# Convolution taps, one product and three groups of TensorE work placed elsewhere in a two-layer mixer

## The chip, the cores and the metric

The kernel runs on one core of one Trainium2 chip. The metric is device time in microseconds (us), as the median of three runs. The engines are TensorE (PE in the profile, with PEld for its weight loads), VectorE (DVE), ScalarE (ACT), GpSimd (POOL) and SyncE (SP), which only issues DMAs here. Each engine works through its own instructions in the order in which the program gives them.

## What is computed

256 tokens of width 1024 go through two layers of a first block and one layer of a second. A layer of the first block is, cut to what matters here:

```
x = x + 0.5 * swiglu(rms_norm(x))                    # feed-forward, width 2816
proj = rms_norm(x) @ w_in
y_rwkv = rwkv7(token_shift(proj[:, :1280]))           # 6 heads of 64: a recurrence over tokens
y_attn = dilated_attention(q, k, v)                   # 6 heads, blocks of 128 keys
y_conv = conv(u)                                      # 256 channels
x = x + concat(y_rwkv, y_attn, y_conv) @ w_out
x = x + 0.5 * swiglu(rms_norm(x))

conv:  z = u[:, :256] * sigmoid(u[:, 256:])
       z = depthwise convolution of z, 31 taps, + bias      # causal, over tokens
       z = (z - mean(z)) * rsqrt(var(z) + 1e-5) * ln_w + ln_b
       y = silu(z)

rwkv7: state = state * w + (state @ -kk) x (kk * a) + v x k ;  y = state @ r     # for each token
       then a norm over each head, a bonus term, a gate
```

All of it is float32. The second block (attention, a short convolution, pooling, feed-forward) is not touched.

## The kernel before

A float32 product runs on TensorE as three passes: each weight piece of 128 x 1024 is loaded by SyncE (`raw`), copied by ScalarE into `hi` (L287), and VectorE makes `lo = raw - hi` (L288). A product is then `hi*xh + lo*xh + hi*xl`. There are three `raw` buffers and six each of `hi` and `lo`, so a piece's `hi` can only be written once TensorE has done with the piece six before it.

Inside a layer's mixer (`mixers`, L793) the token recurrence is turned into products over two chunks of 128 tokens. For each chunk and head a triangular system has to be solved. It is done in 16 x 16 blocks first (`substitute`, L1001): 15 steps of three small VectorE instructions each, a shuffle (L1004), a product (L1005) and a sum (L1007), each needing the one before. The result `X16` goes through ScalarE into `X32` (L1070, L1071) and through VectorE's transpose into `Y32` (L1072), and TensorE then joins the blocks into 32 x 32, 64 x 64 and 128 x 128 systems (`XM`, `A16`, `A32`, `A64`, `Yf`). In front of the substitution stand the products `Bt` and AR (L975 to L977) and their scores (L990), which make the system's matrix `XM`.

TensorE's gaps between these dependent pieces are filled with matmuls of the large projections. Each projection is a generator in the list `jobs`; `run(n)` (L810) advances it by n steps, of three matmuls each (`mm` in the profile). While the mixer is emitted, TensorE's matmuls are pinned to the order of the code (`pinned`, `tc.keep_in_program_order`). The order on VectorE, ScalarE, GpSimd and SyncE is not pinned: a scheduler chooses it by its own estimate of when operands are ready.

Names that the change touches, with their lines before:

- `taps(j)` (L865): for each of the two halves of the convolution's channels, 30 VectorE instructions (L869) that add one tap each to `ca[j]`, each needing the one before, with a ScalarE instruction at each end (L867, L870). The code calls it late (L1260), but its input `z` is ready early, so the scheduler spreads the taps over VectorE.
- `km` (L1075), a product of 128 x 768 on VectorE, and `Kt` (L1076), which is made of it.
- `turned(...)` (L1111): three transposes on TensorE of the values `vT`, copied by ScalarE to `Vt`. `vT` is written by VectorE at L841. `rv_of(0)` (L1163) multiplies `ka[0]` by `Vt`.
- `AR[:, :, :, 1]` (L1198), the receptance part; the scores `kr[0]` (L1230) need it.
- the convolution's tail: the channel sum `cs` (L1261), `csq` (L1268), `token_rsqrt` of it (L1285, with its power on GpSimd), `spread` over the tokens (L1293), and the tanh gate that gives `mix[6]` and `mix[7]`. The fourth output projection step group, `ojob(3)`, is the first that reads `mix[6]`.
- in the feed-forward (`Grouped.go`, L556): the hidden values of one column group are turned by TensorE (`turning`, L571) between the steps of the next group.

Of the kernel before, what the change touches and what calls it, by code (L numbers as in the profile page):

```python
# [14 lines left out]
OP = mybir.AluOpType  # L15

T, DM, ND = 256, 1024, 8
# [168 lines left out]
def tile_model(ctx, tc, A, at, out):  # L186
# [113 lines left out]
    def both(calls):  # L300

        for i, c in enumerate(calls):
            m = pe.matmul(*c[:3], start=c[3], stop=c[3] if len(c) < 5 else c[4], skip_group_check=True)
            if i or pinned[0]:
                tc.keep_in_program_order(m)

    def turn(ps, src):

        placed(pe.transpose(ps, src, ident))  # L309
# [200 lines left out]
    class Grouped:  # L510
# [45 lines left out]
        def go(self, finish, nxt, aside=None):  # L556
# [45 lines left out]
            for g, (c0, m) in enumerate(GROUPS):  # L602
                if g:

                    b, hs = self.space(m), []
                    t = turning(h, 512, hs)
                    for i, _ in enumerate(self.cols(b, m)):
                        if (i if m == 512 else i - 2) >= 0:
                            next(t, None)
                    for _ in t:  # L610
                        pass
                    s = silu(b, m)
                    if g == 2 and aside:
                        aside()
                    if m == 512:
                        downs(hs, g == 1)
# [176 lines left out]
    def mixers(me, finish, nxt):  # L793
        l, lpk, hl = me.l, me.lpk, me.nrm.hl

        def lpar(name, i=0, n=1, p0=0, p1=128):
            o, w = at[1][name]
            return lpk[p0:p1, o + i:o + i + n]
# [66 lines left out]
        def taps(j):  # L865
            ca[j] = tmp.tile([128, T], F32, name="ca", bufs=2)
            act.activation(ca[j], z[:, j, 30:], AF.Identity, scale=lpar("taps", j * TAPS + 30))  # L867
            for k in range(30):
                dve.scalar_tensor_tensor(ca[j], z[:, j, k:k + T], lpar("taps", j * TAPS + k), ca[j], op0=OP.mult, op1=OP.add)  # L869
            act.activation(ca[j], ca[j], AF.Identity, scale=0.5, bias=lpar("conv_dw_b", j))  # L870
# [115 lines left out]

        run(16)
        XM = [n6(t3("XM")) for c in range(2)]
# [9 lines left out]
        dve.tensor_scalar(N16, N32[:, :, 0:16], m0, None, op0=OP.mult)  # L998
        dve.scalar_tensor_tensor(N16, N32[:, :, 16:32], m1, N16, op0=OP.mult, op1=OP.add)

# [70 lines left out]
        act.activation(X32[:, :, 16:32], X16, AF.Copy, scale=m1)  # L1071
        dve.transpose(Y32, X32)  # L1072
        run(4)
        qk_spread(k_, 1.0, rbk)
        dve.tensor_tensor(km_[:, :768], km_[:, :768], kT_[:, :768], op=OP.mult)  # L1075
        dve.tensor_tensor(c4(Kt_), c4(km_), Ei[:, :, :, 1:129], op=OP.mult)  # L1076
# [61 lines left out]
        run(8)  # L1138
        turned(lambda f: vT[:, f, 0:128], Vt[:, 0])
        mix[3] = at_[0].out(vtok)  # L1140
# [11 lines left out]
        run(8)  # L1152
        turned(lambda f: vT[:, f, 128:256], Vt[:, 1])

# [8 lines left out]
        def rv_of(c):  # L1163
            b = bank("at")
            both([(b[:, hc], ka[c][:, h], Vt[:, c, hc], h == 0) for h, f, p, hc in heads])
            act.activation(Rv[c], b[:, :384], AF.Copy)

        rv_of(0)
        run(8)
        at_[1].turns()  # L1170
# [94 lines left out]
        for j in range(2):  # L1265
            dve.scalar_tensor_tensor(ca[j], cs[:, :T], -1.0 / 256, ca[j], op0=OP.mult, op1=OP.add)
            csq.append(t1("csq"))
            act.activation(csq[j], ca[j], AF.Square)  # L1268
        run(4)

        yc_ = u3("yc"); yc = v3(yc_)
# [8 lines left out]
        run(4)  # L1280
        b2 = bank("at")
        for j in range(2):
            for c in range(2):
                mm(b2[:, c:c + 1], csq[j][:, c * 128:c * 128 + 128], ones[:, 0:1], j == 0 and c == 0, j == 1)
        rc = token_rsqrt(b2[:, :2], 2, 1.0 / 256, 1e-5, "nc")  # L1285
        run(2)
        b = bank("at")
        head_sums(b, [ysq[:, f] for f in range(3)])
        rb_ = t3("rby"); rb = rb_[:, :768].rearrange("p (c n) -> p c n", c=2)
        head_rsqrt(b, 6, 1.0 / 64, 64e-5, rb, "nr")  # L1290
        run(2)
        rs = bank("at")[:, :T]
        spread(rs, rc)  # L1293
        for j in range(2):
# [5 lines left out]
            dve.scalar_tensor_tensor(yb, th, 1.0, yb, op0=OP.add, op1=OP.mult)  # L1300
            mix[6 + j] = split(yb, 0.5)

        Dc_ = u3("Dc"); Dc = v3(Dc_)
# [10 lines left out]
        dve.tensor_tensor(yc_[:, :768], yc_[:, :768], gw_[:, :768], op=OP.mult)  # L1314
        run(6)
        for f, ps in enumerate(spread3(rb)):
# [256 lines left out]
```

## Time and profile before

| what | value |
|---|---|
| device time, median of 3 runs | 1443.67 us (1442.15 to 1444.58) |
| the profiled execution's own time | 1440.27 us |
| its span, first to last instruction | 1438.5 us |
| mean granted TensorE clock | 0.971 |
| TensorE busy | 1373.0 us, 95% |
| VectorE busy | 887.7 us, 62% |
| ScalarE busy | 773.5 us, 54% |
| GpSimd busy | 59.7 us, 4% |

The shares are averages over stages. TensorE's idle time and its lowered clock stand almost wholly in two places, around 200 to 390 us and 760 to 940 us: the mixers of the two layers. The times of the two mixers agree within 0.1 us wait for wait, so the rows further down are of the first; the second layer's stand 556 us later. "Granted clock" is the share of full speed that the throttle allows: 1.00 is 2.4 GHz and 0.50 is 1.2 GHz. In a timeline the first column is the start, the second the duration, and the bracket at the end gives the idle time of that engine before the instruction and what ended it.

### The profile page before, as it was taken

How to read it: one execution, taken by the hardware profiler on the slowest of the kernel's cores; microseconds unless marked ns; L12 is line 12 of the kernel's file. 1: busy time of each engine (PE TensorE's matmuls, PEld its weight loads, DVE VectorE, ACT ScalarE, POOL GpSimd, SP SyncE). 2: the span in 40 equal slices, each digit the busy share in tenths (PEclk: the TensorE clock that was granted, in tenths of full speed). 3: DMA queues.
4: the chain of work that ended last, by engine and by line, in shares of the span. 5: the costliest groups of instructions: out<-in, count | busy, mean ns of one | idle time of the engine just before them, and what ended most of it. 6: DMA issues, size and time to landing. Idle time of an engine off the chain costs nothing. (4 is left out here: it accounts for less than half of the span.)

```text
span 1438.5 us, 24789 instructions
## 1 busy us (share of the span) xinstructions
PE 1373.0 (95%) x10034; PEld 1252.5 (87%) x10034; DVE 887.7 (62%) x1450; ACT 773.5 (54%) x1251; POOL 59.7 (4%) x72
## 2 busy tenths in 40 slices
PE   9999999689999999999999869999999999899997
PEld 7888999588888889888898859888889988899997
DVE  6555477865754656545566885664545556777765
ACT  5544455464643545444446545554444487766664
POOL 1000012000100000000002200110000000000000
PEclk9999999789999999999999969999999999999998
DMA  7756563321565764665663522266665534566551
GB/s 238 228 185 183 182 201 111 106 82 52 161 191 176 231 195 152 214 182 186 190 194 115 152 72 64 98 204 182 188 183 183 177 121 149 158 178 176 176 176 44
DMA packets 68658, 231.41 MB, mean 161 GB/s; under 512 B 7704, under 2 KB 12480, under 8 KB 68544
## 3 DMA queue, kind: packets, MB, share of 16 engines
q1 hardware_dynamic: 68544, 229.83, 52.0%
q8 instruction: 78, 1.28, 0.4%
q14 instruction: 36, 0.29, 0.1%
HBM read 227.69 MB, written 2.11 MB: 160 GB/s over the span
## 5 line engine op out<-in xcount | busy, mean ns | idle before, releaser
L288 DVE TENSOR_TENSOR lo<-raw,hi 128x1024 fp32r<-128x1024 f32 (+1 forms) x388 | 473.9, 1223 | 370.7 <-ACT hi L287 369.6
L287 ACT ACTIVATE hi<-raw 128x1024 fp32r<-128x1024 f32 (+1 forms) x388 | 407.7, 1054 | 450.5 <-PE at L298 204.4
L298 PE MATMUL mm<-hl,hi 128*128 128x256 f32 x880 | 248.9, 283 | 1.7 <-DVE hl L665 1.2
L298 PE MATMUL mm<-hh,lo 128*128 128x256 f32 x880 | 247.2, 281 | 0.0
L298 PE MATMUL mm<-hh,hi 128*128 128x256 f32 x880 | 247.1, 282 | 0.0
L298 PE MATMUL at<-hi,xh 128*128 128x512 f32 (+1 forms) x768 | 231.2, 382 | 0.1
L298 PE MATMUL at<-lo,xh 128*128 128x512 f32 (+1 forms) x768 | 224.0, 373 | 0.2
L298 PE MATMUL at<-hi,xl 128*128 128x512 f32 (+1 forms) x768 | 223.9, 373 | 0.0
L298 PEld LDWEIGHTS mm<-hl,hi 128*128 128x128 f32 x880 | 166.0, 189 | 5.5 <-DVE hl L665 4.7
L298 PEld LDWEIGHTS mm<-hh,hi 128*128 128x128 f32 x880 | 166.0, 189 | 1.6 <-issue 0.4
L298 PEld LDWEIGHTS mm<-hh,lo 128*128 128x128 f32 x880 | 166.2, 189 | 0.0
L298 PEld LDWEIGHTS at<-lo,xh 128*128 128x128 f32 x768 | 139.7, 188 | 27.4 <-DVE lo L398 1.3
L298 PEld LDWEIGHTS at<-hi,xl 128*128 128x128 f32 x768 | 140.0, 188 | 26.0
L298 PE MATMUL mm<-xh,hi 128*128 128x256 f32 x512 | 154.2, 301 | 2.5 <-ACT xh L481 2.5
L298 PEld LDWEIGHTS at<-hi,xh 128*128 128x128 f32 x768 | 132.8, 189 | 18.6 <-ACT hi L397 0.9
L298 PE MATMUL mm<-xl,hi 128*128 128x256 f32 x512 | 148.2, 289 | 0.5 <-DVE xl L482 0.5
L298 PE MATMUL mm<-xh,lo 128*128 128x256 f32 x512 | 147.9, 289 | 0.0
L298 PE MATMUL at<-xh,hi 128*128 128x256 f32 x432 | 123.1, 286 | 1.5 <-ACT xh L1521 1.5
L298 PE MATMUL at<-xl,hi 128*128 128x256 f32 x432 | 123.0, 286 | 0.6 <-DVE xl L425 0.6
L298 PE MATMUL at<-xh,lo 128*128 128x256 f32 x432 | 122.3, 284 | 0.0
L298 PEld LDWEIGHTS mm<-xh,hi 128*128 128x128 f32 x512 | 101.3, 198 | 7.4 <-ACT xh L481 3.3
L298 PEld LDWEIGHTS mm<-xl,hi 128*128 128x128 f32 x512 | 101.2, 198 | 2.1 <-DVE xl L482 0.9
(310 smaller groups left out, 1788.7 us busy)
## 6 DMA issues: line engine op xcount, KB each, us to landing
raw<-ffn SPq DMA_DIRECT2D x326, 512.0 KB, 3.6
raw<-win SPq DMA_DIRECT2D x60, 512.0 KB, 3.8
raw<-wout SPq DMA_DIRECT2D x24, 512.0 KB, 3.6
raw<-win SPq DMA_DIRECT2D x8, 384.0 KB, 3.1
raw<-ffn SPq DMA_DIRECT2D x8, 256.0 KB, 4.8
bias<-dbias SPq DMA_DIRECT2D x12, 128.0 KB, 2.2
lpk<-pack SPq DMA_DIRECT2D x2, 625.0 KB, 4.9
rows<-ebd SPq DMA_DIRECT2D x16, 64.0 KB, 2.8
```

The costliest lines, as they stand in the source:

```text
L287: act.activation(hi[:, :n], raw[:, :n], AF.Copy)
L288: dve.tensor_sub(lo[:, :n], raw[:, :n], hi[:, :n].bitcast(F32))
L298: placed(pe.matmul(out, lhsT, rhs, start=start, stop=stop, skip_group_check=True))
```

## The change

Five edits:

1. In the feed-forward, the transposes of the hidden values start two steps later in column group 1 and one step later in group 5.
2. The scores that make `XM` come after 18 steps of the projections instead of 16; the two steps come out of those that follow.
3. `behind(i, first)` gives the scheduler an order without a semaphore: the first tap of each half behind the transpose `Y32`, and the `km` product behind `N16`, the last preparation of the substitution.
4. The two `turned` calls of the values move one `run(8)` on, and `rv_of(0)` with its `run(8)` moves behind the second.
5. The sums of the convolution's squares and their factor move ahead of the head means of the recurrence; the head factor `rby` moves behind the convolution's gate, and two `run(2)` become part of a `run(9)`.

```diff
@@ -304,6 +304,11 @@
             if i or pinned[0]:
                 tc.keep_in_program_order(m)
 
+    def behind(i, first):
+
+        tc.add_manual_dep(i.ins, first.ins.name, mybir.DependencyInfo(mybir.DependencyClass.NoSync, mybir.DependencyReason.DATA),
+                          reason="behind")
+
     def turn(ps, src):
 
         placed(pe.transpose(ps, src, ident))
@@ -605,7 +610,7 @@
                     b, hs = self.space(m), []
                     t = turning(h, 512, hs)
                     for i, _ in enumerate(self.cols(b, m)):
-                        if (i if m == 512 else i - 2) >= 0:
+                        if i >= {1: 2, 5: 3}.get(g, 0):
                             next(t, None)
                     for _ in t:
                         pass
@@ -866,7 +871,9 @@
             ca[j] = tmp.tile([128, T], F32, name="ca", bufs=2)
             act.activation(ca[j], z[:, j, 30:], AF.Identity, scale=lpar("taps", j * TAPS + 30))
             for k in range(30):
-                dve.scalar_tensor_tensor(ca[j], z[:, j, k:k + T], lpar("taps", j * TAPS + k), ca[j], op0=OP.mult, op1=OP.add)
+                t = dve.scalar_tensor_tensor(ca[j], z[:, j, k:k + T], lpar("taps", j * TAPS + k), ca[j], op0=OP.mult, op1=OP.add)
+                if k == 0:
+                    behind(t, y32)
             act.activation(ca[j], ca[j], AF.Identity, scale=0.5, bias=lpar("conv_dw_b", j))
 
         def vjob():
@@ -984,7 +991,7 @@
             for hh in range(2):
                 dve.tensor_tensor(dst[:, hh::2], b[hh], smask[:, mk, None, :].to_broadcast([128, 3, 128]), op=OP.mult)
 
-        run(16)
+        run(18)
         XM = [n6(t3("XM")) for c in range(2)]
         for c in range(2):
             scores(c, Bt, 0, 0, XM[c])
@@ -996,7 +1003,7 @@
                 dve.transpose(N32[q, c * 6:c * 6 + 6], XM[c][q, :, q])
         N16 = i16("N16")
         dve.tensor_scalar(N16, N32[:, :, 0:16], m0, None, op0=OP.mult)
-        dve.scalar_tensor_tensor(N16, N32[:, :, 16:32], m1, N16, op0=OP.mult, op1=OP.add)
+        n16 = dve.scalar_tensor_tensor(N16, N32[:, :, 16:32], m1, N16, op0=OP.mult, op1=OP.add)
 
         def substitute():
             for s in range(15):
@@ -1069,10 +1076,10 @@
         X32, Y32 = half("X32", 12), half("Y32", 12)
         act.activation(X32[:, :, 0:16], X16, AF.Copy, scale=m0)
         act.activation(X32[:, :, 16:32], X16, AF.Copy, scale=m1)
-        dve.transpose(Y32, X32)
+        y32 = dve.transpose(Y32, X32)
         run(4)
         qk_spread(k_, 1.0, rbk)
-        dve.tensor_tensor(km_[:, :768], km_[:, :768], kT_[:, :768], op=OP.mult)
+        behind(dve.tensor_tensor(km_[:, :768], km_[:, :768], kT_[:, :768], op=OP.mult), n16)
         dve.tensor_tensor(c4(Kt_), c4(km_), Ei[:, :, :, 1:129], op=OP.mult)
         run(2)
         dbias = lambda h: A["dbias"][:, h * T:h * T + T]
@@ -1136,7 +1143,6 @@
             for q in qs:
                 act.activation(Yf[c][q, :, q], Y32[q, c * 6:c * 6 + 6], AF.Copy)
         run(8)
-        turned(lambda f: vT[:, f, 0:128], Vt[:, 0])
         mix[3] = at_[0].out(vtok)
         att_scores(1)
 
@@ -1150,7 +1156,7 @@
             act.activation(Yf[c][0:32, :, 32:64], b[0:32, c * 6:c * 6 + 6], AF.Copy)
             act.activation(Yf[c][64:96, :, 96:128], b[64:96, c * 6:c * 6 + 6], AF.Copy)
         run(8)
-        turned(lambda f: vT[:, f, 128:256], Vt[:, 1])
+        turned(lambda f: vT[:, f, 0:128], Vt[:, 0])
 
         for c in range(2):
             b = bank("at")[:, :384].rearrange("p (n j) -> p n j", n=6)
@@ -1165,8 +1171,9 @@
             both([(b[:, hc], ka[c][:, h], Vt[:, c, hc], h == 0) for h, f, p, hc in heads])
             act.activation(Rv[c], b[:, :384], AF.Copy)
 
+        run(8)
+        turned(lambda f: vT[:, f, 128:256], Vt[:, 1])
         rv_of(0)
-        run(8)
         at_[1].turns()
         for c in range(2):
             b = bank("at")[:, :384].rearrange("p (n j) -> p n j", n=6)
@@ -1267,6 +1274,11 @@
             csq.append(t1("csq"))
             act.activation(csq[j], ca[j], AF.Square)
         run(4)
+        b2 = bank("at")
+        for j in range(2):
+            for c in range(2):
+                mm(b2[:, c:c + 1], csq[j][:, c * 128:c * 128 + 128], ones[:, 0:1], j == 0 and c == 0, j == 1)
+        rc = token_rsqrt(b2[:, :2], 2, 1.0 / 256, 1e-5, "nc")
 
         yc_ = u3("yc"); yc = v3(yc_)
         ysq_ = t3("ysq"); ysq = v3(ysq_)
@@ -1278,17 +1290,6 @@
             dve.scalar_tensor_tensor(yc[:, f], ps[f], -1.0 / 64, yT[:, f], op0=OP.mult, op1=OP.add)
             act.activation(ysq[:, f], yc[:, f], AF.Square)
         run(4)
-        b2 = bank("at")
-        for j in range(2):
-            for c in range(2):
-                mm(b2[:, c:c + 1], csq[j][:, c * 128:c * 128 + 128], ones[:, 0:1], j == 0 and c == 0, j == 1)
-        rc = token_rsqrt(b2[:, :2], 2, 1.0 / 256, 1e-5, "nc")
-        run(2)
-        b = bank("at")
-        head_sums(b, [ysq[:, f] for f in range(3)])
-        rb_ = t3("rby"); rb = rb_[:, :768].rearrange("p (c n) -> p c n", c=2)
-        head_rsqrt(b, 6, 1.0 / 64, 64e-5, rb, "nr")
-        run(2)
         rs = bank("at")[:, :T]
         spread(rs, rc)
         for j in range(2):
@@ -1299,6 +1300,10 @@
             act.activation(th, yb, AF.Tanh, scale=0.5)
             dve.scalar_tensor_tensor(yb, th, 1.0, yb, op0=OP.add, op1=OP.mult)
             mix[6 + j] = split(yb, 0.5)
+        b = bank("at")
+        head_sums(b, [ysq[:, f] for f in range(3)])
+        rb_ = t3("rby"); rb = rb_[:, :768].rearrange("p (c n) -> p c n", c=2)
+        head_rsqrt(b, 6, 1.0 / 64, 64e-5, rb, "nr")
 
         Dc_ = u3("Dc"); Dc = v3(Dc_)
         gw_ = u3("gw"); gw = v3(gw_)
@@ -1312,7 +1317,7 @@
             dve.scalar_tensor_tensor(Dc[:, f], Dc[:, f], lpar("rwkv_ln_b", f), b[:, T:2 * T], op0=OP.add, op1=OP.mult)
             act.activation(gw[:, f], b[:, T:2 * T], AF.Identity, scale=lpar("rwkv_ln_w", f))
         dve.tensor_tensor(yc_[:, :768], yc_[:, :768], gw_[:, :768], op=OP.mult)
-        run(6)
+        run(9)
         for f, ps in enumerate(spread3(rb)):
             dve.tensor_tensor(yc[:, f], ps, yc[:, f], op=OP.mult)
             dve.tensor_tensor(yc[:, f], yc[:, f], Dc[:, f], op=OP.add)
```

Edit 3 shows on VectorE. At the end of the substitution (`X` is `X16`, `tb` its scratch, `ca` the taps), before:

```order
L1004 STREAM_SHUFFLE tb<-X_2103 128x12x14
L869 SCALAR_TENSOR_TENSOR ca<-z,lpk,ca 128x256
L1005 TENSOR_TENSOR tb<-tb,N_2365 128x12x14
L869 SCALAR_TENSOR_TENSOR ca<-z,lpk,ca 128x256
L1007 TENSOR_TENSOR X_2103<-X_2103,tb 128x12x14
L869 SCALAR_TENSOR_TENSOR ca<-z,lpk,ca 128x256
L1004 STREAM_SHUFFLE tb<-X_2103 128x12x15
L869 SCALAR_TENSOR_TENSOR ca<-z,lpk,ca 128x256
L1005 TENSOR_TENSOR tb<-tb,N_2365 128x12x15
L869 SCALAR_TENSOR_TENSOR ca<-z,lpk,ca 128x256
L1007 TENSOR_TENSOR X_2103<-X_2103,tb 128x12x15
L869 SCALAR_TENSOR_TENSOR ca<-z,lpk,ca 128x256 x3
```

and now, where line numbers are 7 higher for the substitution and 5 higher for the taps:

```order
L1011 STREAM_SHUFFLE tb<-X_2103 128x12x13
L288 TENSOR_TENSOR lo<-raw,hi 128x1024
L1012 TENSOR_TENSOR tb<-tb,N_2377 128x12x13
L288 TENSOR_TENSOR lo<-raw,hi 128x1024
L1014 TENSOR_TENSOR X_2103<-X_2103,tb 128x12x13
L1011 STREAM_SHUFFLE tb<-X_2103 128x12x14
L1012 TENSOR_TENSOR tb<-tb,N_2377 128x12x14
L1014 TENSOR_TENSOR X_2103<-X_2103,tb 128x12x14
L1011 STREAM_SHUFFLE tb<-X_2103 128x12x15
L1012 TENSOR_TENSOR tb<-tb,N_2377 128x12x15
L1014 TENSOR_TENSOR X_2103<-X_2103,tb 128x12x15
L1079 STREAM_TRANSPOSE Y_2670<-X_2669 128x384
```

The taps between the small instructions are gone; the first seven of them stand behind the transpose. Two weight splits (`lo`) stand between the small instructions instead, as others did before.

Further on VectorE, ahead of AR's second half (`r` is the receptance, `raws` its projection as it leaves PSUM), before:

```order
L836 TENSOR_TENSOR raws<-mm,R 128x2x256
L288 TENSOR_TENSOR lo<-raw,hi 128x1024
L841 SCALAR_TENSOR_TENSOR r<-raws,omu,m_3243 128x256
L841 SCALAR_TENSOR_TENSOR r<-raws,omu,m_3246 128x256
L836 TENSOR_TENSOR raws<-mm,R 128x256
L288 TENSOR_TENSOR lo<-raw,hi 128x1024
L841 SCALAR_TENSOR_TENSOR r<-raws,omu,m_3330 128x256
L479 TENSOR_TENSOR xl<-at,xh 128x256
L1198 TENSOR_TENSOR AR<-r,E 128x6x128
```

and now:

```order
L874 SCALAR_TENSOR_TENSOR ca<-z,lpk,ca 128x256 x2
L841 TENSOR_TENSOR raws<-mm,R 128x2x256
L874 SCALAR_TENSOR_TENSOR ca<-z,lpk,ca 128x256
L288 TENSOR_TENSOR lo<-raw,hi 128x1024
L846 SCALAR_TENSOR_TENSOR r<-raws,omu,m_3230 128x256
L846 SCALAR_TENSOR_TENSOR r<-raws,omu,m_3233 128x256
L874 SCALAR_TENSOR_TENSOR ca<-z,lpk,ca 128x256 x12
L841 TENSOR_TENSOR raws<-mm,R 128x256
L874 SCALAR_TENSOR_TENSOR ca<-z,lpk,ca 128x256 x2
L846 SCALAR_TENSOR_TENSOR r<-raws,omu,m_3330 128x256
L484 TENSOR_TENSOR xl<-at,xh 128x256
L1205 TENSOR_TENSOR AR<-r,E 128x6x128
```

Of the 60 taps of a layer, 15 stand in this piece now and none before.

Edit 4 shows on TensorE. Behind the last step of the projection of the values (`pk` with `v` is the transpose), before:

```order
L298 MATMUL mm<-xh,hi 128x256
L298 MATMUL mm<-xl,hi 128x256
L298 MATMUL mm<-xh,lo 128x256
L309 MATMUL at<-pk,v 128x128 x3
L303 MATMUL at<-PT,va 64x256 x2
L303 MATMUL at<-PT,va 64x128 x2
L303 MATMUL at<-ka,q 128x128 x2
L303 MATMUL at<-ka,q 128x256 x2
```

and now, at the same place:

```order
L298 MATMUL mm<-xh,hi 128x256
L298 MATMUL mm<-xl,hi 128x256
L298 MATMUL mm<-xh,lo 128x256
L303 MATMUL at<-PT,va 64x256 x2
L303 MATMUL at<-PT,va 64x128 x2
L303 MATMUL at<-ka,q 128x128 x2
L303 MATMUL at<-ka,q 128x256 x2
```

with the first transposes eight steps later, in front of the 64 x 64 systems:

```order
L298 MATMUL mm<-xl,hi 128x256
L298 MATMUL mm<-xh,lo 128x256
L314 MATMUL at<-pk,v 128x128 x3
L298 MATMUL at<-XA,XM 64x64 x12
L303 MATMUL at<-AR,Kt 128x128 x6
```

The attention output (`PT,va`) and the next scores (`ka,q`) follow the projection directly; the first transposes come behind the 32 x 32 systems and 24 more matmuls of a projection.

## Rows read from the trace of the kernel before

**Rows 1.** The page, part 1: busy us, share, instructions.

```profile
PE 1373.0 (95%) x10034; PEld 1252.5 (87%) x10034; DVE 887.7 (62%) x1450; ACT 773.5 (54%) x1251; POOL 59.7 (4%) x72
```

**Rows 2.** Waits of TensorE, whole span: line, what it waited for, us, times, longest.

```profile
PE at L298 <- ACT X L1070: 28.1, 2, 14.0
PE at L309 <- DVE v L841: 8.4, 2, 4.2
PE at L303 <- DVE Bt L976: 4.3, 2, 2.2
...
PE at L309 <- DVE sg L568: 2.3, 2, 1.6
```

**Rows 3.** Timeline of TensorE, 225 to 296 us: start, us, what, [idle before, releaser].

```profile
234.26 2.78 PE L303 MATMUL at<-AR,Bt 64*128 64x128 f32 x24 [2.16 <-DVE Bt L976]
...
280.21 1.48 PE L298 MATMUL at<-X,XM 32*32 32x16 f32 x96 [14.03 <-ACT X L1070]
```

**Rows 4.** Windows, TensorE alone: stretch, us, PE busy (instructions), granted clock, DMA.

```profile
230.02:231.82 1.80, 1.80 (x17) 1.00 0.00 0
...
234.30:237.90 3.60, 3.60 (x28) 0.53 0.28 56
...
280.20:285.50 5.30, 5.29 (x115) 0.50 0.04 8
...
300.50:309.60 9.10, 9.05 (x108) 0.50 0.40 143
...
353.80:360.50 6.70, 5.28 (x19) 0.75 0.07 11
```

**Rows 5.** Timeline of ScalarE, 225 to 330 us.

```profile
262.44 2.00 ACT L287 ACTIVATE hi<-raw 128x1024 fp32r<-128x1024 f32 x2
...
279.70 0.45 ACT L1070 ACTIVATE X<-X,pk 128x192 f32<-128x192 f32 x1 [12.72 <-DVE X L1007]
```

**Rows 6.** Groups of VectorE, 243.2 to 279.7 us: instructions, busy, mean ns, idle before.

```profile
L869 DVE SCALAR_TENSOR_TENSOR ca<-z,lpk,ca 128x256 f32<-128x256 f32 x30 | 14.2, 474 | 0.0
L288 DVE TENSOR_TENSOR lo<-raw,hi 128x1024 fp32r<-128x1024 f32 (+1 forms) x9 | 10.2, 1130 | 4.1 <-ACT hi L287 4.1
L1004 DVE STREAM_SHUFFLE tb<-X 128x12 f32<-128x12 f32 (+14 forms) x15 | 4.2, 277 | 0.0
...
L1007 DVE TENSOR_TENSOR X<-X,tb 128x12 f32<-128x12 f32 (+14 forms) x15 | 3.8, 250 | 0.0
```

**Rows 7.** Timeline of VectorE, 236 to 290 us.

```profile
243.28 0.21 DVE L1004 STREAM_SHUFFLE tb<-X 128x12 f32<-128x12 f32 x1
...
271.18 0.28 DVE L1005 TENSOR_TENSOR tb<-tb,N 128x132 f32<-128x132 f32 x1
271.38 0.47 DVE L869 SCALAR_TENSOR_TENSOR ca<-z,lpk,ca 128x256 f32<-128x256 f32 x1
271.78 0.28 DVE L1007 TENSOR_TENSOR X<-X,tb 128x132 f32<-128x132 f32 x1
...
281.27 2.40 DVE L869 SCALAR_TENSOR_TENSOR ca<-z,lpk,ca 128x256 f32<-128x256 f32 x5
```

**Rows 8.** Timeline of VectorE, 212 to 237 us.

```profile
228.24 0.96 DVE L1075 TENSOR_TENSOR km<-km,k 128x768 f32<-128x768 f32 x1 [2.13 <-ACT km L960]
```

**Rows 9.** Timeline of TensorE, 296 to 372 us.

```profile
300.55 0.48 PE L309 MATMUL at<-pk,v 128*128 128x128 f32 x1 [4.18 <-DVE v L841]
...
329.15 0.94 PE L303 MATMUL at<-AR,Kt 64*128 64x128 f32 x12
...
359.96 0.38 PE L298 MATMUL mm<-xh,hi 128*128 128x256 f32 x1 [1.27 <-ACT xh L481]
```

**Rows 10.** Windows, all engines: PE, PEld, DVE, ACT, POOL busy, clock, DMA.

```profile
279.70:300.50 20.80, 16.16 (x334) 14.74 (x334) 18.87 (x46) 14.65 (x36) 0.11 (x1) 0.83 0.15 43
300.50:327.90 27.40, 27.31 (x288) 24.10 (x289) 13.03 (x32) 15.63 (x38) 0.58 (x5) 0.83 0.26 86
327.90:346.40 18.50, 18.50 (x202) 16.35 (x202) 11.08 (x30) 8.49 (x23) 0.00 (x0) 1.00 0.24 72
```

## The prediction, made before the changed kernel was run

> **What bounds the kernel now.** I read the page's first part first. TensorE is busy 95% of the span and every other engine at most 62% [rows 1], so time is lost only where TensorE waits or runs slowly. The list of TensorE's waits comes next: the largest are two waits each (one a layer) of 14.0 us for `X32`, 4.2 us for `v` and 2.2 us for `Bt`, with a small one for the feed-forward's `sg` [rows 2]. TensorE's timeline puts them at their places [rows 3, 9]. The windows show what follows each: right behind the wait the granted clock is about 0.5, the lower of the two levels, for 3.6, 5.3 and 9.1 us [rows 4]. So a wait costs itself and part of the slow stretch behind it. Last I ask who is late: `X32` follows ScalarE's wait for VectorE's `X16` [rows 5], and VectorE from the first shuffle at 243.28 (the second instruction of the substitution's stretch, [rows 7]) to 279.7, where ScalarE takes `X16` over [rows 5], has no idle time but 4.1 us for `hi` [rows 6]. The stretch holds 45 small instructions (15 each of 4.2, 3.8 and, as long as the sums, 3.8 us of products, 11.8), 30 taps (14.2 us) and other work.
>
> The sums below are for one layer, made against the profiled execution (1440.27 us) and doubled; the median of the runs, 1443.67, lies 3.4 above it, and the saving is taken off that.
>
> **Bt and its scores (edits 2 and 3).** The `km` product stands in VectorE's queue ahead of `Bt` at 0.96 us [rows 8], and now stands behind N16. Two projection steps (six matmuls of 0.12, as 17, those at both ends in part, take 1.80 us at full clock [rows 4]: 0.7 us) fill TensorE's wait before the scores. With the 0.3 that the queue behind `km` gives, an estimate, 2.0 of the 2.16 us [rows 3] go, bounds 0.7 and 2.16. The 3.6 us at clock 0.53 [rows 4] hold 1.9 us of work at full speed, so 1.7 us were lost; I take 1.5 back. Sum 3.5. It moves TensorE forward, but ahead of the wait for `X32` that is worth nothing by itself: the sum for the stretch up to X32's use is set by VectorE's chain alone.
>
> **The chain to X32 (edit 3).** Before, it takes 36.4 us. A tap costs the chain less than its 0.47 us: with a tap between, two dependent small instructions start 0.60 apart (271.18 to 271.78 [rows 7]), the tap starting 0.20 behind the first and the next small one 0.40 behind the tap. Alone they last 0.25 to 0.28 [rows 6, 7], and I add 0.03 for the hand-over, which makes 0.31. So a tap gives back 0.29, not 0.47; 29 taps go, 8.4 us. A single `km` product comes in and one weight split of 768 goes out ahead, which cancel. Of the 4.1 us idle for `hi` [rows 6] I keep 0.5: TensorE is 3.3 earlier by the part above and frees the `hi` buffers earlier, so the `hi` pair that ScalarE writes at 262.44 [rows 5] ends near 261. That alone would make 36.4 - 8.4 - 3.6 = 24.4. Built up instead from what is left (45 small ones 11.8 plus 45 x 0.03; 8 splits of about 1.1, and `q`, `ka`, `km`, `Kt` and smaller ones, 12.9 together; 0.5 idle; 1.3 off where an independent one overlaps) it is 25.2. I take 25.2. It starts 0.3 earlier, since the queue ahead is full and loses little. `X32` is used 11.45 earlier, at 268.75 instead of 280.21 [rows 3].
>
> TensorE reaches that place at 280.21 - 14.03 = 266.2 before, 3.3 earlier now, 262.9. It still waits 5.9 us instead of 14.0, and the slow 5.3 us behind [rows 4] stay. The two parts together are worth 11.45. Bounds: 8.4 with no idle time saved and the start not moved, 13.4 if the built-up sum is two too long.
>
> The Trainium skill ("VectorE: DVE Perf Modes", section "The DRAIN you can't avoid") says that a next operation does not start until the pipe has emptied, and that a semaphore adds nothing between chained ones. By that rule a tap gives back its whole pitch of 0.40, and 29 of them 11.6 instead of 8.4. The rows speak against a full drain: five dependent taps take 2.40, 0.48 each [rows 7], while the independent small one starts 0.40 behind a tap. As whatever is saved ahead of the last `hi` only lengthens the idle time there, the rule would add 1.2 us a layer at most (11 taps by 0.11).
>
> **The taps' new places and the values turned later (edits 3 and 4).** The 4.18 us wait for `v` [rows 9] is passed over: TensorE goes on with the attention output, the scores, the 32 x 32 systems and 24 matmuls, and the transposes come after `v` is there. That is worth 4.2, and 4.5 of the slow 9.1 us behind [rows 4]: 8.7.
>
> But the taps have to go somewhere. Counted in the order, VectorE has 24 taps between `Y32` and the last `v` where 19 were (seven right behind `Y32`, of which the five at 281.27 [rows 7] were there before), 5 x 0.48 = 2.4 us more, and 27 between the last `v` and AR's second half where 9 were, 18 x 0.48 = 8.7 us more. VectorE was busy 18.87 of 20.80 us up to the turn of `v`, 13.03 of the 27.40 up to AR, and 11.08 of the 18.50 behind [rows 10]. Of the first 2.4 us 1.9 find idle time, and `v`, half a microsecond late, is asked for later than that. The next stretch becomes 0.5 + 13.0 + 8.7 = 22.2 us of VectorE work: AR starts at 322.7 and, at 0.96, as `km` takes for the same size [rows 8], ends at 323.65, on the clock that counts from 300.5. TensorE asks for the scores of AR and `Kt` at 329.15 before [rows 9], now 8.7 earlier, 320.45. A new wait of 3.2 us, and by the slow stretches above half of as long a stretch behind it is lost, 1.6. Net: 8.7 - 4.8 = 3.9. Bounds: 0, if `v` or another value in this queue is as late as the whole gain, and 8.7, if the scheduler's taps fall into VectorE's idle time. The last nine taps have 7.4 us idle in the stretch behind AR [rows 10], 9 x 0.48 = 4.3, and don't count.
>
> **The convolution's tail (edit 5).** TensorE waits 1.27 us for `xh` of `mix[6]` [rows 9], and the clock stands at 0.75 in the 6.7 us around it [rows 4], 1.7 us lost. The factor is now ready before the head means, so `mix[6]` comes earlier by several steps; the tanh gate's work is the same. Against it: the head factor `rby` now comes behind the gate, covered by the `run(9)`. I take 2.0, bounds 0.8 (part of the wait stays) and 3.0.
>
> **Feed-forward (edit 1).** The transposes' waits for `sg` are 2.3 us in the whole span [rows 2]. The longest is 1.6, and up to two further steps, each of several matmuls of 0.12 [rows 4], now stand in front of the transposes: 2.3 go, lower bound 0.
>
> **The sum.** 11.45 + 3.9 + 2.0 = 17.35 a layer, 34.7 for two, and 2.3: 37.0. The profiled execution would take 1440.3 - 37.0 = 1403.3, the median 1443.7 - 37.0 = 1406.7. This forecast's own range is 1400 to 1413.
>
> **Rivals.**
>
> *VectorE binds behind X32.* The taps taken out of the chain delay `v`, AR and what follows by as much as TensorE gains there. For it: VectorE was 91% busy (18.87 of 20.80) up to `v` and gets five taps more, and 18.87 us contain waits that the order can turn into queueing. Against it: 14.4 us idle before AR. The gains of edits 4 and 5 are lost: 2 x 11.45 + 2.3 = 25.2, median 1418.5.
>
> *No new wait.* VectorE's work between `v` and AR is done ahead, since its queue runs before TensorE; AR is ready at 320, and the slow stretch of the convolution goes wholly. For it: 14.4 us idle in 27.4. Against it: the sum 22.2 above ends after TensorE's arrival. 2 x (11.45 + 8.7 + 3.0) + 2.3 = 48.6, median 1395.
>
> *The pipe's drain*, as weighed above: 2 x 1.2 more than my forecast, 1404.3.
>
> *Slower: the taps are the bound wherever they stand.* All 29 come to stand in front of something that TensorE needs, none in idle time: 14.5 us at 0.5 behind X32 against 11.45 won ahead of it, 3.05 more a layer, less the 2.3 of the feed-forward: 1447.5. It decides from 25 of the 29 taps on the path (25.2 / 2 / 0.5). Against it: VectorE has 1.9 + 14.4 + 7.4 = 23.7 us idle in the 66.7 behind X32 [rows 10].
>
> *The order has no effect on the chip,* because `X16` waits for something other than the taps: `hi` at 262.44 plus what follows it. Then 1443.7. Against it: the idle time for `hi` is 4.1 of 36.4 us.
>
> **Chances.** Forecast 0.52, VectorE binds 0.22, no new wait 0.15, the drain 0.05, slower 0.04, no effect 0.02. Faster by over 0.2% (2.9 us, about what a measurement of this kernel can tell from no change) is the first four, 0.94; the same 0.02; slower 0.04. The range that holds 8 in 10 takes half of the "no new wait" cases and most of "VectorE binds": 1393 to 1424.
>
> **What would show it.** In the changed kernel's profile the wait for `X32` is near 6 us a layer instead of 14.0 and the stretch from the first shuffle to the end of `X16` near 25 us; `v` and `Bt` are gone from the list of TensorE's waits; a new wait for AR of about 3 us stands at the scores of AR and `Kt`; the clock is 1.00 behind the scores of `Bt` and at the former place of the turn of `v`, and still 0.5 behind `X32`; the wait for `xh` at the output projection is gone. The forecast is wrong where the wait for AR is 6 us or more, or the wait for `v` only moves on (VectorE binds), where no such wait appears (no new wait), or where the chain to `X32` stays above 30 us.

## The result, and the profile after

The changed kernel takes 1406.66 us (median of 4 runs, 1404.39 to 1409.49) against 1443.15 us (4 runs, 1442.15 to 1444.58): ratio 0.9747, 95% interval 0.9727 to 0.9767, so 34 to 39 us less. The forecast was 1406.7. The agreement is closer than the steps behind it: for the profiled execution the same sum gave 1403.3, and the changed kernel's profiled execution took 1406.87. The profiled spans differ by 33.4 us (1438.5 and 1405.1), 3.6 less than the 37.0 of the sum.

TensorE's waits in the whole span (line, what it waited for; us, times, longest), to be held against [rows 2]:

```profile
PE at L298 <- ACT X L1077: 12.1, 2, 6.1
PE at L303 <- ACT Yf L1157: 4.3, 2, 2.2
PE at L314 <- ACT rba L1044: 2.8, 4, 1.3
...
PE at L314 <- DVE sg L573: 0.6, 1, 0.6
...
PE at L303 <- DVE Bt L983: 0.3, 1, 0.3
```

`v` is gone, `Bt` is 0.3, the wait for `X32` is 6.1 where the forecast said 5.9. There is no wait for AR. In its place stands one that I did not foresee, for ScalarE's `Yf`, and one for `rba` (the factors of the attention's `q` and `k`). TensorE's timeline in the first mixer, as [rows 3, 9]:

```profile
233.81 1.61 PE L303 MATMUL at<-AR,Bt 64*128 64x128 f32 x24 [0.29 <-DVE Bt L983]
...
251.51 0.33 PE L314 MATMUL at<-pk,rba 128*128 128x128 f32 x1 [1.26 <-ACT rba L1044]
...
270.68 1.48 PE L298 MATMUL at<-X,XM 32*32 32x16 f32 x96 [6.06 <-ACT X L1077]
...
296.37 2.13 PE L303 MATMUL at<-AR,Kt 64*128 64x128 f32 x12 [2.15 <-ACT Yf L1157]
...
315.42 0.94 PE L303 MATMUL at<-AR,Kt 64*128 64x128 f32 x12
```

The scores of `Bt` wait 0.29 us where they waited 2.16; the product with `X32` comes at 270.68 instead of 280.21, though the mixer itself begins 0.7 us later in this execution; the scores of AR and `Kt` at 315.42 start at once. The product at 296.37 doesn't read `Yf`: by the code it writes one of the PSUM buffers (`at`) that take turns, and the profile has it released by the copy of `Yf`, so it waits until ScalarE has emptied the buffer that it is to write. Where the clock stands lower, as [rows 4] (stretch, length, busy and instructions, granted clock):

```profile
233.80:237.40 3.60, 3.60 (x41) 1.00 0.28 51
270.70:276.00 5.30, 5.30 (x115) 0.50 0.10 33
...
296.40:300.40 4.00, 3.97 (x21) 0.57 0.06 23
334.00:346.00 12.00, 11.93 (x87) 1.00 0.14 45
```

Behind `Bt` the clock is now 1.00, behind `X32` still 0.50, behind the new wait for `Yf` 0.57, and around the convolution's tail 1.00 where it was 0.75.

For the comparison of all runs I cut each mixer by four of TensorE's own instructions: from the decay product (`lpk`, `aug`) to the first product with `X32` (A), to the product of `U` and `BK` right behind the scores of AR (B), to the channel sum of `ca` (C), and to the first matmul of the next feed-forward (D). The mean of the two layers, in us:

| kernel | A | B | C | D | sum | median of runs |
|---|---|---|---|---|---|---|
| before | 66.1 | 49.9 | 15.3 | 28.9 | 160.1 | 1443.15 |
| changed | 55.7 | 45.8 | 15.5 | 25.65 | 142.7 | 1406.66 |
| taps bound, nothing else | 57.4 | 48.95 | 15.3 | 28.9 | 150.5 | 1421.69 |
| changed, taps not bound | 64.0 | 44.7 | 15.3 | 25.65 | 149.7 | 1421.58 |
| changed, km not bound | 56.1 | 46.6 | 15.5 | 25.65 | 143.8 | 1408.97 |
| changed, XA's memset later | 54.0 | 46.0 | 15.5 | 25.65 | 141.2 | 1403.63 |
| changed, Yf before the softmax | 55.8 | 44.9 | 16.2 | 25.6 | 142.6 | 1404.81 |
| changed, halves in turn | 55.8 | 45.6 | 15.7 | 26.2 | 143.3 | 1406.26 |
| XA later, three splits behind X | 50.7 | 44.1 | 15.7 | 29.7 | 140.2 | 1399.93 |
| XA later, two splits behind X | 52.3 | 45.5 | 15.2 | 27.1 | 140.2 | 1400.34 |
| three splits, channel sum later | 50.5 | 44.8 | 19.3 | 24.5 | 139.2 | 1397.99 |

The two layers of one kernel agree within 1.3 us in the sum. A mixer is 17.4 us shorter, two 34.9; the other 1.5 us of the spans were lost outside: the first mixer begins 0.7 us later, and the work behind the second mixer, which no edit but the first touches, takes 508.9 us instead of 508.0. In the profiles of the twelve kernels that last part varies between 507.8 and 509.5.

The kernels were run in several groups, each with the kernel before beside it (medians 1443.15, 1442.47, 1443.44 and 1441.49). So kernels are best compared by their ratio to the kernel before, which is given with its 95% interval, and by the stretches of the table. The changed kernel's ratio is 0.9747, 0.9727 to 0.9767.

### The profile page after: what moved, and what is told of

It is laid out like the page before. It is cut to its first block, busy times and chain, and to the rows that moved or that the text cites. A ratio compares the mean times of both kernels' runs of the same rounds, so it can differ in the third digit from the quotient of the medians.

```text
span 1405.1 us, 24784 instructions
## 1 busy us (share of the span) xinstructions
PE 1364.3 (97%) x10034; PEld 1247.7 (89%) x10034; DVE 890.7 (63%) x1450; ACT 772.7 (55%) x1251; POOL 59.7 (4%) x72
## 5 line engine op out<-in xcount | busy, mean ns | idle before, releaser
L298 PEld LDWEIGHTS at<-lo,xh 128*128 128x128 f32 x768 | 139.9, 189 | 27.1 <-DVE lo L403 1.1
```

The source lines that it names most:

```text
L298: placed(pe.matmul(out, lhsT, rhs, start=start, stop=stop, skip_group_check=True))
```

## The experiments

**Are the taps the chain?** The kernel before with the one edit, and the changed kernel without it (this diff and those below show only the lines that matter):

```diff
             for k in range(30):
-                dve.scalar_tensor_tensor(ca[j], z[:, j, k:k + T], ...)
+                t = dve.scalar_tensor_tensor(ca[j], z[:, j, k:k + T], ...)
+                if k == 0:
+                    behind(t, y32)
```

> The kernel before, with only the taps bound behind Y32 (half of edit 3). Theory (the chain on VectorE sets X32's use, the taps later find idle time): X32 is used 10 to 11 us earlier a layer, TensorE's wait for it falls from 14.0 to 3 to 4 us, the wait for v stays at 4 to 5, no wait for AR; gain 20 to 22 us, near 1422. Rival (VectorE binds wherever the taps stand): the waits for v and AR grow by what X32 gains; 1435 or more.

> The changed kernel without the binding of the taps. Theory (the parts add up): wait for X32 about 16 to 17 us a layer, since only TensorE comes earlier; the values turned later give 4 us a layer and the convolution's tail 3; near 1428, and the gains of this kernel and of the one with the taps alone add up to that of the change. Rival (the other edits pay only once the chain is short): 1436 or more.

Measured: 1421.69 us (ratio to the kernel before 0.9861, 0.9845 to 0.9877) and 1421.58 (0.9865, 0.9841 to 0.9889). The first time is the theory's, though `X32` is used 8.7 us earlier (A) and not 10 to 11, and its wait is 5.7 and not 3 to 4. VectorE does not bind behind `X32`: the wait for `v` even falls to 3.9. TensorE's waits with the taps alone bound, and then in the changed kernel without that binding:

```profile
PE at L298 <- ACT X L1077: 11.4, 2, 5.7
PE at L314 <- DVE v L846: 7.6, 2, 3.9
```

```profile
PE at L298 <- ACT X L1075: 28.1, 2, 14.0
...
PE at L303 <- ACT Yf L1155: 2.2, 2, 1.1
```

The second came out 6 us better than I expected: without the binding the wait for `X32` is 14.0, not 16 to 17, since `X32` itself comes 2.1 us earlier (A). VectorE's idle time for `hi` in the chain is 2.4 us there instead of 4.1, probably because TensorE, earlier by `Bt`, frees the buffers earlier; no run separates this. The two gains of 20.8 and 20.9 add up to 41.7, and the change brings 36.5: a layer loses 2.6 us of the sum, 2.0 of them in B, where TensorE waits 2.2 us for `Yf` with both and 1.1 with the taps not bound.

What a tap costs the chain can be read here without the other edits: VectorE's splits between the first shuffle and the last sum, the first shuffle, and ScalarE taking `X16` over, all with the taps alone bound.

```profile
L288 DVE TENSOR_TENSOR lo<-raw,hi 128x1024 fp32r<-128x1024 f32 (+1 forms) x9 | 10.2, 1131 | 3.1 <-ACT hi L287 3.1
...
244.38 0.20 DVE L1011 STREAM_SHUFFLE tb<-X 128x12 f32<-128x12 f32 x1
...
272.16 0.46 ACT L1077 ACTIVATE X<-X,pk 128x192 f32<-128x192 f32 x1 [4.39 <-DVE X L1014]
```

The chain is 27.8 us (244.38 to 272.16) where it was 36.4, and its idle time 3.1 where it was 4.1 [rows 6]. So 29 taps gave back 8.6 - 1.0 = 7.6 us, 0.26 each. The forecast had 0.29. The rival by which a tap gives back its whole 0.40 falls.

**What is left of the chain: km, XA and `rba`.** The changed kernel's chain ends at 270.17, 26.5 us after its first shuffle at 243.70 (forecast 25.2), and has 1.9 us idle where the forecast left 0.5. VectorE's splits in the chain, `X16` taken over by ScalarE, and then GpSimd and ScalarE in front of that, in the changed kernel:

```profile
L288 DVE TENSOR_TENSOR lo<-raw,hi 128x1024 fp32r<-128x1024 f32 (+1 forms) x8 | 9.2, 1152 | 1.9 <-ACT hi L287 1.9
...
270.17 0.46 ACT L1077 ACTIVATE X<-X,pk 128x192 f32<-128x192 f32 x1 [4.48 <-DVE X L1014]
```

```profile
247.07 0.73 POOL L1130 MEMSET XA<- 64x768 f32 x1 [9.83 <-DVE Kt L1083]
247.76 3.04 POOL L325 TENSOR_TENSOR ny<-nv,mhalf 128x12 f32<-128x12 f32 x1
...
250.84 1.12 ACT L1044 ACTIVATE rba<-ny 128x384 f32<-128x384 f32 x2 [5.08 <-POOL ny L325]
251.87 1.04 ACT L287 ACTIVATE hi<-raw 128x1024 fp32r<-128x1024 f32 x1
```

GpSimd's memset of `XA` (the matrix in which the 64 x 64 systems are put together) waits for VectorE's `Kt`; `Kt` comes late because `km` stands in front of it; and the power for `rba` stands behind the memset, though its own input was ready at 245.8. ScalarE waits 5 us for it, with the next `hi` behind `rba` in its queue, and VectorE's split waits for that `hi`. (`km`'s former place is in [rows 8].) Two ways to take it away:

```diff
# km not bound
-        behind(dve.tensor_tensor(km_..., op=OP.mult), n16)
+        dve.tensor_tensor(km_..., op=OP.mult)
# XA later (pows collects the powers of rsqrt)
-        pool.memset(X64, 0.0)
+        behind(pool.memset(X64, 0.0), pows[-1])
```

> The changed kernel without the binding of km. Theory (km behind N16 makes Kt late, GpSimd's memset of XA waits for Kt, and the power for rba stands behind that memset): the wait for rba falls from 1.3 to about 0.2, VectorE's idle time for hi from 1.9 to about 0.5, X32 is used about 1.2 us earlier a layer though Bt's wait comes back to 1 us; 1404 to 1405. Rival (my forecast's step, km's place is worth 0.3 us on the chain): 1407 to 1408.

> The changed kernel with GpSimd's memset of XA placed behind the two powers for rba. Theory (as above): the wait for rba falls to 0.3 or less, Bt's stays at 0.3, X32 is used 1.2 us earlier a layer; 1404 to 1405. Rival (the power itself is what takes longer, 3.0 instead of 2.3 us): the wait for rba stays at 0.7 or more and the time at 1406 to 1407.

Measured: 1408.97 (0.9771, 0.9752 to 0.979), 1.0 above the rival's range, and 1403.63 (0.9733, 0.9716 to 0.9749), 0.4 below the theory's. Both intervals overlap with that of the changed kernel, so the stretches have to decide. Without the binding `Bt` is late again (1.4 us of wait), A is 0.4 longer, about the size that the forecast gave to `km`'s place (0.3), and B 0.8. The memset is then done (245.86 to 246.59) before the power's input is there, as the theory said, but nothing is won by it: another queue takes its place. ScalarE comes late to the power's input `nv`, since the `hi` in front of it waits 3.5 us for the DMA of its weights, and VectorE's idle time for `hi` stays at 1.9:

```profile
246.67 0.84 ACT L287 ACTIVATE hi<-raw 128x768 fp32r<-128x768 f32 x1 [3.50 <-DMA raw<-win]
247.42 0.58 ACT L1040 ACTIVATE nv<-at,eps,r 128x6 f32<-128x6 f32 x2
...
248.09 2.92 POOL L325 TENSOR_TENSOR ny<-nv,mhalf 128x12 f32<-128x12 f32 x1 [1.49 <-ACT nv L1040]
```

With the memset moved the power starts as soon as its input is there, and VectorE's splits in the chain wait less:

```profile
244.51 2.33 POOL L326 TENSOR_TENSOR ny<-nv,mhalf 128x12 f32<-128x12 f32 x1 [8.61 <-ACT nv L1041]
...
256.85 0.73 POOL L1131 MEMSET XA<- 64x768 f32 x1
...
L288 DVE TENSOR_TENSOR lo<-raw,hi 128x1024 fp32r<-128x1024 f32 (+1 forms) x8 | 9.2, 1152 | 0.4 <-ACT hi L287 0.4
```

The waits for `rba` are gone, VectorE's idle time for `hi` in the chain is 0.4, and A is 1.7 us shorter. So 1.7 us that an earlier TensorE could have won stayed in a queue on GpSimd that I had not looked at. What `km`'s new place is worth by itself, a few tenths of a microsecond, is not told apart from the other things that move with it.

**Why no wait for AR?** I had two suspects: the size of a tap, and ScalarE's queue in front of it.

```diff
# halves in turn
                 if k == 0:
                     behind(t, y32)
+                    if j:
+                        behind(t, lasttap[-1])
+                lasttap.append(t)
# Yf before the softmax
         mix[3] = at_[0].out(vtok)
-        att_scores(1)
 ...
             act.activation(Yf[c][64:96, :, 96:128], ...)
+        att_scores(1)
         run(8)
```

> The changed kernel with the second half's taps placed behind the first half's last one, so that no tap stands between two of the other half. Theory (taps of alternating halves start 0.40 apart, those of one half 0.48; the room before AR is enough for either): groups of taps take 0.48 each instead of 0.40, no wait for AR over 0.5, 1406 to 1408. Rival (my forecast missed the wait for AR only because it sized a tap at 0.48): a wait for AR of 1.5 us or more a layer, 1410 or more.

> The changed kernel with the second attention block's scores issued behind the 32 x 32 systems instead of ahead of them, so that ScalarE copies XA and Yf before it comes to that block's exponentials. Theory (the wait for Yf, 2.2 us a layer, and the half clock behind it are ScalarE's queue: the softmax stands ahead of the copies that free the bank): the wait for Yf falls to 0.3 or less, the stretch from X32's use to the product of U and BK shortens by 3 to 4 us a layer; near 1400. My forecast's wait for AR would then show, since TensorE comes 3 to 4 us earlier: with it 1402 to 1405 and 1 to 3 us of wait for AR. Rival (another copy behind the softmax takes over): the wait moves, 1405 to 1407.

With the halves in turn: 1406.26 (0.974, 0.9721 to 0.9759), no wait for AR, as the theory had it. VectorE in the changed kernel, and then with the halves in turn (AR's product, the last projection of `r`, and the largest group of taps before it):

```profile
305.44 4.83 DVE L874 SCALAR_TENSOR_TENSOR ca<-z,lpk,ca 128x256 f32<-128x256 f32 x12
311.34 0.43 DVE L841 TENSOR_TENSOR raws<-mm,R 128x256 f32<-128x256 f32 x1 [1.07 <-PE mm L298]
...
313.38 0.95 DVE L1205 TENSOR_TENSOR AR<-r,E 128x768 f32<-128x768 f32 x1
```

```profile
303.76 5.16 DVE L876 SCALAR_TENSOR_TENSOR ca<-z,lpk,ca 128x256 f32<-128x256 f32 x10
309.30 0.43 DVE L841 TENSOR_TENSOR raws<-mm,R 128x256 f32<-128x256 f32 x1 [0.38 <-PE mm L298]
...
312.08 0.95 DVE L1210 TENSOR_TENSOR AR<-r,E 128x768 f32<-128x768 f32 x1
```

Twelve taps take 4.83 us in the changed kernel, 0.40 from one to the next; ten of one half take 5.16, 0.52. Both halves are bound to the same instruction, and by these spacings the scheduler alternates them, so that neighbours no longer depend on each other. That was a gain of the change that I did not see, but it did not decide: even at 0.52 AR is ready. The reason is in the second row of each: before AR's chain VectorE waits (1.07 and 0.38 us) for TensorE's own projection of `r`. In the kernel before it waited 4.53 us at this place:

```profile
325.07 0.43 DVE L836 TENSOR_TENSOR raws<-mm,R 128x256 f32<-128x256 f32 x1 [4.53 <-PE mm L298]
```

So the taps filled idle time, and AR follows TensorE: in the profiles of all twelve kernels, in both layers, TensorE asks for the scores of AR and `Kt` 4.08 us after VectorE has begun to take over that projection, and AR is ready 0.35 to 1.09 us before that. No kernel here brings TensorE there as early as the forecast had it (40.2 us after the use of `X32`; the earliest is 43.2), so whether VectorE would then be late is not shown. VectorE's whole stretch from the last `v` to AR, as [rows 10] (third pair its busy time):

```profile
290.50:314.30 23.80, 21.62 (x195) 19.89 (x194) 20.34 (x51) 14.94 (x36) 0.42 (x4) 0.93 0.34 101
```

It was busy 20.34 of 23.80 us, where the forecast had 22.2 without a gap.

With `Yf` copied first: 1404.81 (0.9727, 0.9705 to 0.975), not told apart from the changed kernel and no wait for AR. The wait for `Yf` is gone, and 1.4 us of it now stand as a wait for the copy of `Vt`, which has become the one behind the softmax. TensorE's waits:

```profile
PE at L298 <- ACT X L1077: 12.1, 2, 6.0
...
PE at L303 <- ACT Vt L1122: 2.9, 2, 1.4
```

Of the 2.2 us and the half clock, 0.9 is won in B and 0.7 given back in C, where ScalarE's `U` is late by 0.25; where the rest of the 0.7 goes I have not followed. The wait moved, as the rival said, so the place of one copy alone does not decide. The rows of the changed kernel show what stands in the way: the four normalisations of the softmax, ahead of `Yf` on ScalarE.

```profile
293.85 1.48 ACT L722 ACTIVATE P<-P,rc 128x128 f32<-128x128 f32 x4
295.33 0.32 ACT L1157 ACTIVATE Yf<-at 32x192 f32<-32x192 f32 x1
...
296.00 0.32 ACT L1157 ACTIVATE Yf<-at 32x192 f32<-32x192 f32 x1
```

**The feed-forward's transposes (edit 1).**

```diff
-                        if i >= {1: 2, 5: 3}.get(g, 0):
+                        if (i if m == 512 else i - 2) >= 0:
```

> The changed kernel without edit 1. My forecast's step: 2.3 us longer, near 1409, with the waits for sg back at 2.3. Theory (the waits only moved from sg to hh and hl, 1.9 us in the first feed-forward): the waits for hh and hl in the first feed-forward go, those for sg come back, the time stays within 1 us of 1406.7.

Measured: 1410.09 (1409.70 to 1410.85; ratio 0.9767, 0.9748 to 0.9786), 3.4 us above the changed kernel, with overlapping intervals; the mixers of both are alike, and in the profiles the whole difference stands in the first feed-forward. TensorE with edit 1 undone, and then in the changed kernel:

```profile
35.23 0.69 PE L314 MATMUL at<-pk,sg 128*128 128x128 f32 x2 [2.56 <-DVE sg L573]
```

```profile
34.96 0.42 PE L314 MATMUL at<-pk,sg 128*128 128x128 f32 x2
...
43.80 0.39 PE L298 MATMUL mm<-hh,hi 128*128 128x256 f32 x1 [0.86 <-ACT hh L589]
45.17 0.39 PE L298 MATMUL mm<-hl,hi 128*128 128x256 f32 x1 [0.99 <-DVE hl L590]
```

The waits did move, as my theory after the result said: 2.56 us for `sg` stand against 0.86 and 0.99 for `hh` and `hl`. What it had not counted on is the clock. Behind the wait for `sg` it was low with edit 1 undone, and not at the same place with the taps alone bound, where the feed-forward is as before too (there its wait too; then stretch, length, busy and instructions, granted clock):

```profile
34.30:41.20 6.90, 5.97 (x16) 0.51 0.71 252
```

```profile
PE at L314 <- DVE sg L573: 2.2, 1, 2.2
...
34.30:41.20 6.90, 6.06 (x31) 1.00 0.78 255
```

At 0.51, 6.9 us lose 3.4, as much as the whole difference. Behind the waits of 1.6 and 2.2 us at this place, in the kernel before and with the taps alone bound, the clock stayed at 1.00. From the statistics of the first feed-forward to the decay product it takes 190.8, 191.3 and, with the low clock, 194.9 us in the three profiles with the old places, and 189.9 to 191.8 in those of the nine kernels with the new. So against the kernel before no gain of edit 1 is shown, and 3.4 us where the old places let the clock fall. Whether it fell in the other executions of this kernel too, no profile shows; their times lie within 1.2 us of one another.

**A faster version.** X32 was still the largest wait, and six splits of 1024 stand in its chain. The three kernels have the memset of XA behind the powers too; the edit is given in words.

```diff
+            # in piece(), for the 4th to 6th split issued behind the substitution (two: 5th and 6th)
+            behind(lo, last sum of the substitution)
```

> The changed kernel with the memset of XA behind both powers and, besides, three of the six weight splits of 1024 that stand in the substitution placed behind its last sum. Theory (X32 is set by VectorE's chain, each split costs it 1.1 us and TensorE needs none of these three before X32): X32 used 3.4 us earlier a layer than with the memset alone, its wait near 2.6 instead of 6.0; 6 to 7 us less than that kernel, 1396 to 1398. Rival (the splits are wanted at once behind X32 and hold the raw buffers): TensorE waits for lo, 1402 to 1405.

> As the kernel with three weight splits behind the substitution, with two of them. Theory (VectorE's total load decides at the convolution: each split moved behind X32 pushes the last taps back by its 1.1 us, and the channel sum waits for them): X32 used 2.2 us earlier a layer than with the memset alone, its wait near 3.7, the wait for ca falls from 2.5 to 1.5 or less; near 1399. Rival (the wait for ca comes from the order that the scheduler chose with three): no wait for ca, 1396 to 1397.

> As the kernel with three splits behind the substitution, with the head means of the recurrence and their four steps in front of the convolution's channel sum, and four of the nine steps behind the gate in front of the convolution's spread. Theory (the wait for ca is 2.5 us because the last taps are late, and these steps of TensorE cover 3 us): no wait for ca over 0.3, the half clock behind it gone, 3 to 4 us a layer less than with three splits alone, 1392 to 1394. Rival (the gate and xh of mix[6] are then late at the output projection): a wait for xh of 1 us or more, 1397 or more.

Measured: 1399.93 (0.9698, 0.9678 to 0.9718), 1400.34 (0.9708, 0.9679 to 0.9737) and 1397.99 (0.9703, 0.968 to 0.9726). All three lie below the changed kernel, with two splits by intervals that just overlap; against the memset alone (0.9716 to 0.9749), and from one another, the intervals do not tell them apart. The first and the last missed their theory's numbers (1396 to 1398, and 1392 to 1394). In A the splits give 3.3 and 1.7 us a layer (forecast 3.4 and 2.2), and TensorE does not wait for them. The waits with three splits, with two, and with three and the channel sum later:

```profile
PE at L301 <- ACT X L1083: 5.0, 2, 2.5
PE at L301 <- ACT ca L880: 4.7, 2, 2.5
```

```profile
PE at L301 <- ACT X L1083: 8.2, 2, 4.1
...
PE at L301 <- ACT ca L880: 2.3, 2, 1.2
```

```profile
PE at L301 <- ACT X L1083: 5.0, 2, 2.5
PE mm L301 <- ACT xh L489: 3.1, 2, 1.6
```

Most of what A and B win against the memset alone (5.2 us with three splits, 2.2 with two), D gives back, 4.0 and 1.4: the channel sum waits 2.5 us for `ca` with three splits, 1.2 with two, as if the last taps ended later by what was put in front of them. That is the wait that the forecast feared at AR; it stands at the taps' end. With the sum moved back, `xh` of `mix[6]` is late instead, 1.6 us, as its rival said. This fits a VectorE whose total work behind `X32` is now the limit, so that another order mostly chooses where it shows; no run that takes work off VectorE there tests it.

## Why the prediction was right, and where it was not

- **Bt: right.** 2.16 to 0.29 us, clock behind it 1.00.
- **The chain: right, 1.0 us a layer too much.** A is 10.4 shorter, the forecast 11.45. It started when expected and a tap was worth 0.26, not 0.29; the idle time for `hi` was 1.9 instead of 0.5, by GpSimd's queue. With that queue mended A is 12.1 shorter. The step that failed is the 0.5 us that the forecast kept of the 4.1 us idle for `hi`. The wait for `X32`, 6.1 against 5.9, agrees by two misses: TensorE came to it 2.4 us earlier in the mixer than before (A less the wait, 66.1 - 14.03 and 55.7 - 6.06) where the forecast had 3.3 (its own terms, 2.0 and 1.5, add up to 3.5), held up 1.4 at `rba`, and `X32` itself came 1.0 later than forecast.
- **The values turned later: the sum right, the mechanism wrong.** Forecast 8.7 - 4.8 = 3.9, measured 4.1 in B. By the prediction's own list, "where no such wait appears", it was wrong here: no wait for AR came. VectorE's end of AR was right (43.65 us after the use of `X32`, forecast 43.44). The step that failed is TensorE's arrival at the scores of AR, "now 8.7 earlier, 320.45", and with it the "new wait of 3.2 us". TensorE was held up before, at `Yf`, by 2.2 us and by the half clock of 4.0 us at 0.57 behind it, 3.9 together, and asked for them 44.7 us after the use of `X32` instead of 40.2; and where it came earlier, to 43.2, AR did too, as it hangs on TensorE's projection. The prediction added up VectorE's work to AR without that projection. That the loss at `Yf` and the forecast loss at AR came to nearly the same size is chance.
- **The convolution's tail: right mechanism, too small.** D is 3.2 shorter, C 0.2 longer, so 3.0; forecast 2.0, bounds 0.8 to 3.0. The wait of 1.27 us and the whole 1.7 us of the lower clock went, of which the forecast had taken 2.0.
- **The feed-forward: not shown.** Forecast 2.3. The step that failed is "2.3 go": the waits for `sg` fell from 2.3 to 0.6, but 1.9 came up for `hh` and `hl`, and the first mixer begins 0.7 later. What the edit does show, 3.4 us against its own undoing, is a fallen clock that the kernel before didn't have.
- **Rivals.** VectorE binding behind `X32` did not come (the taps alone gain 20.8). "No new wait" was right that AR would not be waited for and wrong in its time, 1395, since `Yf` took its place. The drain of the pipe falls by 0.26 us a tap; no effect falls by the 36.5 us gained; the slower case fell with the wait for `v`, which did not grow even where `v` was turned early (3.9 us with the taps alone bound).

The total came closer than the steps. For the two mixers 2.1 too much in the chains stands against 2.0 too little at the convolution's tails and 0.4 in B, so that 34.9 were gained where 34.7 were forecast. The 2.3 of the feed-forward did not come, and 1.5 were lost outside the mixers; together, less 0.2 more in the mixers, that is the 3.6 by which the profiled execution missed. That the median meets the forecast to 0.04 us all the same is luck: by the medians the gain was 36.5, by the profiled spans 33.4.

## What to carry to other kernels

- When a chain of small dependent instructions sets the end, count for a filler only what the chain loses by it (here 0.26 of 0.47 us), and look at every other engine's queue that the moved instructions feed: an instruction that waits in order holds back unrelated work behind it, two engines away.
- When a stall goes, the engine arrives at later places earlier by the stall and its slow clock, and the next wait can stand in front of the one that was expected: here it was ScalarE's `Yf`, not VectorE's AR. Look through every engine's queue on the way, not only that of the engine whose work was moved.
- Ask of the last link of a chain what it hangs on. AR stood behind a long row of VectorE's work, but it could not be late by it as long as it waited for TensorE's own projection.
- Work taken out of one chain has an end of its own. With more splits put in front of the taps, TensorE waited at their last user.
- A gain of a few tenths of a percent can be one fallen clock in one stage: look at the windows of both profiles before putting it down to the wait that was moved.

## What the runs showed of the hardware

- Two VectorE instructions of 128 x 256 start 0.40 us apart where the second doesn't need the first, and 0.52 where it does (twelve in 4.83 us, ten in 5.16); the 0.48 that I used was the mean of a mixed group.
- GpSimd's power of 128 x 12 takes 2.3 to 3.0 us for the same work in the rows above, which I cannot explain.
- At the same place of the first feed-forward TensorE's granted clock stayed at 1.00 behind waits of 1.6 and 2.2 us, and was 0.51 for 6.9 us behind one of 2.56.
